# The last group of each block of an input projection: value columns in place of query columns

## The chip, the cores and the metric

The kernel runs on one core of a Trainium2 chip. The metric is the time of one execution in microseconds (us), measured on the device. A difference is called one if it is more than half a per cent, which is about what a measurement of this kernel can tell from no change.

## What is computed

One layer of a decoder, for 256 tokens of width 4096. The part that matters here is the first large product, the input projection: the modulated tokens `u` times a weight matrix of 4096 rows and 11824 columns.

```
mod = c @ w_ada[l] + b_ada[l]
shift, scale, gate = jnp.split(mod, 3, axis=-1)
u = x * (1.0 + scale[:, None]) + shift[:, None]
proj = u @ w_in[l]
(rg_x, rg_g, nsa_q, kv_c, kv_s, kv_w, nsa_gl, nsa_g,
 hg_q, hg_f, hg_i, hg_g) = jnp.split(proj, splits, axis=-1)
...
y = jnp.concatenate([y_rg, y_nsa, y_hg], axis=-1) @ w_out[l]
x = _layer_norm(ALPHA * x + (1.0 + gate[:, None]) * y, ln_g[l], ln_b[l])
```

The columns of `proj` feed three mixers: a gated recurrence (rg), a sparse attention (nsa; `ks` and `vs`, the halves of `kv_s`, are the keys and values of its selected branch, `nsa_q` its queries) and a linear recurrence (hg). A second product, the output projection, follows, and a layer norm ends the layer.

## The kernel before

**Groups and blocks.** The 4096 rows of the input weights are cut into 32 tiles of 128, and these into ten blocks of 2, 2, 2, 3, 3, 4, 4, 4, 4, 4 tiles (the list `KB`; the text counts blocks 0 to 9). The columns are cut into 46 groups of 256 (one of 304), and the list `GROUPS` sets the order in which every block goes through them: kc, vc, four rg_g, four rg_x, four hg_q, four hg_g, then hg_f and hg_i in turn four times, ks, vs, kw, vw, eight nsa_g, eight nsa_q. A group in a block of n tiles is 6n matmuls on TensorE: two halves, n tiles, and three products, because every fp32 operand is split into a rounded part (`hi`, `uh`) and a rest (`lo`, `ul`). At the end of a group in a block the sum leaves PSUM and is added to the group's sum `acc` in SBUF, by VectorE, or by ScalarE (`ev`) and GpSimd.

**Two layouts.** The last field of a group says how its matmuls are made, in `mm` (line 456). Where it is `"nt"`, the weights are the stationary operand and the tokens move through: `seq = ((wh, uh), (wh, ul), (wl, uh))`. Where it is `"tn"`, the tokens are stationary and the weights move: `seq = ((uh, wh), (uh, wl), (ul, wh))`. Both move 256 columns a matmul. `"tn"` are the four hg_i, vs and vw (304 columns); all other groups are `"nt"`. A row of the profile names the moving operand first: `mm<-uh,hi` is an `"nt"` matmul, `mm<-hi,uh` a `"tn"` one.

**Steps.** `chunks` packs the groups of a block into steps of at most 1024 columns times tiles: four tiles make one group a step, two tiles two groups. A step is one DMA of weights (`raw`), a split into `hi` (ScalarE) and `lo` (GpSimd and VectorE, line 118 for all), and its matmuls. Four buffers each hold raw, `hi` and `lo`, and loads and splits are issued some steps ahead.

**What is woven in.** The modulation vector is computed beside this on VectorE (`ps<-ra,pk,ps`, chunks of `w_ada` by DMA into `ra`), one block ahead, and near the end of each block some 8 to 16 small matmuls (line 394) and a few VectorE operations make the next block's `uh` and `ul`; the block after a change of n needs more of this than its own tiles give time for. In block 9 the work of the mixers (fibers, started by a list of conditions in `run_bg`) is woven in between the matmuls. An attention fiber starts when, among other things, its queries and ks, kw, vs, vw are done. The output projection (line 968) comes after block 9.

Of the kernel before, what the change touches and what calls it, by code (L numbers as in the profile page):

```python
# [45 lines left out]
    + [g for i in range(4) for g in (("hg_f", i, 8752 + 256 * i, 256, "nt"),  # L46
                                     ("hg_i", i, 9776 + 256 * i, 256, "tn"))]
    + [("ks", 0, 4608, 256, "nt"),
       ("vs", 0, 4864, 256, "tn"), ("kw", 0, 5120, 256, "nt"), ("vw", 0, 5376, 304, "tn")]
    + [("nsa_g", i, 5680 + 256 * i, 256, "nt") for i in range(8)]  # L50
    + [("nsa_q", i, 2048 + 256 * i, 256, "nt") for i in range(8)]
)
SILU = ("rg_g", "hg_q", "hg_g", "nsa_g")

# [1347 lines left out]
```

## Time and profile before

| | us |
|---|---|
| median of 3 runs | 1672.43 |
| lowest, highest | 1669.08, 1676.03 |
| profiled execution | 1667.61 |
| its span | 1665.9 |
| TensorE busy in the span | 1605.8 (96%) |
| VectorE, ScalarE, GpSimd busy | 1331.2, 972.0, 954.4 |

The profiled execution is one run that the hardware profiler took; its span, from the first instruction to the last, is 1.7 us shorter than its time, and the time is 4.82 us below the median of the runs. Durations are read from it. Matmuls overlap, so that one shown as 281 ns starts some 118 ns after the one before it; what a matmul costs is the distance from start to start.

### The profile page before, as it was taken

To read this page: it belongs to the slowest core of one execution; us is meant where nothing else is said; L and a number is where in the kernel's file an instruction comes from. 1 tells how busy PE (TensorE), PEld (TensorE's weight loads), DVE (VectorE), ACT (ScalarE), POOL (GpSimd) and SP (SyncE) were. 2 spreads that over 40 slices of the span, in tenths; PEclk is the share of its full clock that TensorE was granted. 3 is DMA by queue.
4 is the path that set the end of the run, shared out by engine and by line. 5 is a ranking of instruction groups with operands and counts; after the bars stand their busy time and mean duration, and the time that the engine had idled before them with its cause. 6 is when DMAs were issued, how large, how long until landed. Compare 5 with 4: busy or idle time off the path is not lost.

```text
span 1665.9 us, 33159 instructions
## 1 busy us (share of the span) xinstructions
PE 1605.8 (96%) x11752; PEld 1506.7 (90%) x11752; DVE 1331.2 (80%) x2301; ACT 972.0 (58%) x1557; POOL 954.4 (57%) x765
## 2 busy tenths in 40 slices
PE   4999999999999999999999999889999999999997
PEld 4999999999999999999999999889988888878884
DVE  5668988789888778787777787899679688968875
ACT  2887666665655555555555566664566565655562
POOL 1478987876655555554554555567543444555555
PEclk9999999999999999999999998999999999999999
DMA  8998989999999898898889886767666666689983
GB/s 283 368 334 315 359 302 333 308 349 352 320 348 333 292 343 311 310 330 318 314 323 320 321 310 210 248 237 258 249 216 244 236 215 210 212 292 366 343 332 137
DMA packets 146486, 491.49 MB, mean 295 GB/s; under 512 B 16264, under 2 KB 17288, under 8 KB 146320
## 3 DMA queue, kind: packets, MB, share of 16 engines
q1 hardware_dynamic: 146320, 489.38, 82.5%
q8 instruction: 92, 1.51, 0.4%
q14 instruction: 74, 0.61, 0.1%
HBM read 485.12 MB, written 4.19 MB: 294 GB/s over the span
## 4 chain that ended last, share of the span: by engine, by line
PE 81%; DVE 10%; DMA 3%; ACT 3%; issue 3%; POOL 0%; SPq 0%; DVEq 0%; ACTq 0%; POOLq 0%
PE mm L456 51%; PE mm L968 21%; DVE ps L118 3%; DVE acc L118 2%; DVE lo L118 2%; DMA ra<-in_w_ada_dram 1%; ACT hi L118 1%; PE ps L707 1%; DVE rgt L118 1%; PE ps L900 1%; PE ps L394 1%; PE ps L791 1%; PE ps L1286 1%; DVE hgA L118 1%; DMA raw<-in_w_in_dram 1%
## 5 line engine op out<-in xcount | busy, mean ns | idle before, releaser
L118 POOL TENSOR_TENSOR lo<-raw,hi 128x576 fp32r<-128x576 f32 (+4 forms) x527 | 707.4, 1344 | 620.3 <-ACT hi L118 594.2
L118 ACT CAST hi<-raw 128x1024 fp32r<-128x1024 f32 (+3 forms) x527 | 528.0, 1002 | 495.1 <-POOL lo L118 232.4
L456 PE MATMUL mm<-uh,hi 128*128 128x256 f32 x2560 | 723.5, 283 | 15.0 <-DVE lo L118 8.9
L456 PE MATMUL mm<-uh,lo 128*128 128x256 f32 x2560 | 717.7, 280 | 1.9 <-DVE lo L118 1.4
L456 PE MATMUL mm<-ul,hi 128*128 128x256 f32 x2560 | 717.4, 280 | 0.0
L118 DVE SCALAR_TENSOR_TENSOR ps<-ra,pk,ps 128x512 f32<-128x512 f32 x744 | 520.4, 727 | 8.3 <-DMA ra<-in_w_ada_dram 2.4
L456 PEld LDWEIGHTS mm<-uh,hi 128*128 128x128 f32 x2560 | 485.0, 189 | 19.2 <-DVE lo L118 11.9
L118 DVE TENSOR_TENSOR lo<-raw,ps 128x448 fp32r<-128x448 f32 (+4 forms) x500 | 303.0, 606 | 233.8 <-ACT ps L118 183.0
L456 PEld LDWEIGHTS mm<-ul,hi 128*128 128x128 f32 x2560 | 488.5, 191 | 0.3 <-issue 0.2
L456 PEld LDWEIGHTS mm<-uh,lo 128*128 128x128 f32 x2560 | 484.6, 189 | 2.6 <-DVE lo L118 1.9
L118 ACT CAST ps<-raw 128x448 fp32r<-128x448 f32 (+4 forms) x500 | 260.1, 520 | 6.8 <-DVE acc L118 6.0
L118 DVE TENSOR_TENSOR acc<-mm,acc 128x512 f32<-128x512 f32 (+1 forms) x346 | 231.1, 668 | 0.0
L968 PE MATMUL mm<-hi,yh 128*128 128x512 f32 x512 | 210.8, 412 | 0.3 <-ACT ev L118 0.3
L968 PE MATMUL mm<-hi,yl 128*128 128x512 f32 x512 | 201.3, 393 | 0.0
L968 PE MATMUL mm<-lo,yh 128*128 128x512 f32 x512 | 200.1, 391 | 0.0
L968 PEld LDWEIGHTS mm<-hi,yh 128*128 128x128 f32 x512 | 96.4, 188 | 23.3 <-issue 5.7
L968 PEld LDWEIGHTS mm<-hi,yl 128*128 128x128 f32 x512 | 96.1, 188 | 21.5
L456 PE MATMUL mm<-hi,uh 128*128 128x256 f32 (+1 forms) x384 | 110.4, 288 | 4.3 <-ACT hi L118 3.0
L968 PEld LDWEIGHTS mm<-lo,yh 128*128 128x128 f32 x512 | 96.5, 188 | 19.2 <-issue 1.2
L456 PE MATMUL mm<-hi,ul 128*128 128x256 f32 (+1 forms) x384 | 108.9, 284 | 0.0
L456 PE MATMUL mm<-lo,uh 128*128 128x256 f32 (+1 forms) x384 | 108.8, 283 | 0.0
L118 POOL TENSOR_TENSOR acc<-ev,acc 128x512 f32<-128x512 f32 x77 | 101.4, 1317 | 2.7 <-ACT ev L118 2.3
(193 smaller groups left out, 1474.6 us busy)
## 6 DMA issues: line engine op xcount, KB each, us to landing
ra<-in_w_ada_dram SPq DMA_DIRECT2D x323, 512.0 KB, 5.5
raw<-in_w_in_dram SPq DMA_DIRECT2D x291, 512.0 KB, 4.8
raw<-in_w_out_dram SPq DMA_DIRECT2D x128, 512.0 KB, 4.7
raw<-in_w_in_dram SPq DMA_DIRECT2D x90, 384.0 KB, 5.0
ra<-in_w_ada_dram SPq DMA_DIRECT2D x64, 384.0 KB, 5.4
ra<-in_w_dram SPq DMA_DIRECT2D x16, 512.0 KB, 3.8
raw<-in_w_ada_dram SPq DMA_DIRECT2D x13, 512.0 KB, 6.1
xz<-in_xz_dram SPq DMA_DIRECT2D x16, 256.0 KB, 5.8
```

What stands on the lines that cost most here:

```text
L118: return f(*a, **k)
L394: nc.tensor.matmul(pp[:, q:q + 1], lhsT=acc[q], rhs=ones[:, 0:1], start=kb > 0, stop=True, skip_group_check=kb == 0)
L456: nc.tensor.matmul(dst, lhsT=l_, rhs=r_, start=s and n_ == 0, stop=e and n_ == 2)
L707: nc.tensor.matmul(pl[:, (2 * x + j) * 64:(2 * x + j + 1) * 64], lhsT=k[:, j, x * P:(x + 1) * P], rhs=qp[:, j, x * P:(x + 1) * P].rearrang ...
L791: nc.tensor.matmul(s1[:, b * T:(b + 1) * T], lhsT=q[:, j, P:], rhs=kk[b][:, g], start=True, stop=True)
L900: nc.tensor.matmul(o, lhsT=v0, rhs=eT[:, 0:2], start=b == 0, stop=False)
L968: nc.tensor.matmul(state[x], lhsT=a_, rhs=b_, start=ci == 0 and j == 0 and n_ == 0, stop=ci == len(part) - 1 and j == 1 and n_ == 2)
L1286: nc.tensor.matmul(pb, lhsT=rows[-1 - x], rhs=rows[i // 2][:, i % 2 * 512:i % 2 * 512 + 512], start=True, stop=True)
```

## The change

In `GROUPS`, vs moves from place 28 of each block to place 46, the last, and the eighth group of queries, nsa_q 7, takes place 28. The rows of all other groups, and all code, stay. The host lays the weights out in the new order, so that the loads stay in line.

```diff
     + [("ks", 0, 4608, 256, "nt"),
-       ("vs", 0, 4864, 256, "tn"), ("kw", 0, 5120, 256, "nt"), ("vw", 0, 5376, 304, "tn")]
+       ("nsa_q", 7, 2048 + 256 * 7, 256, "nt"), ("kw", 0, 5120, 256, "nt"), ("vw", 0, 5376, 304, "tn")]
     + [("nsa_g", i, 5680 + 256 * i, 256, "nt") for i in range(8)]
-    + [("nsa_q", i, 2048 + 256 * i, 256, "nt") for i in range(8)]
+    + [("nsa_q", i, 2048 + 256 * i, 256, "nt") for i in range(7)]
+    + [("vs", 0, 4864, 256, "tn")]
```

Lines behind it are numbered one higher in the changed kernel. On TensorE the two places read as follows; the numbers behind the names are buffers. First the end of the 28th group of block 6 and the start of the 29th, kw, before:

```order
L456 MATMUL mm_9275<-hi_9153,uh_8157 128x256
L456 MATMUL mm_9275<-lo_9154,uh_8157 128x256
L456 MATMUL mm_9275<-hi_9153,ul_8158 128x256
L456 MATMUL mm_9314<-uh_8114,hi_9188 128x256
L456 MATMUL mm_9314<-ul_8115,hi_9188 128x256
L456 MATMUL mm_9314<-uh_8114,lo_9189 128x256
```

The same place in the changed kernel:

```order
L457 MATMUL mm_9275<-uh_8157,hi_9153 128x256
L457 MATMUL mm_9275<-ul_8158,hi_9153 128x256
L457 MATMUL mm_9275<-uh_8157,lo_9154 128x256
L457 MATMUL mm_9314<-uh_8114,hi_9188 128x256
L457 MATMUL mm_9314<-ul_8115,hi_9188 128x256
L457 MATMUL mm_9314<-uh_8114,lo_9189 128x256
```

Before, the layout turned from `"tn"` back to `"nt"` here; now it is `"nt"` on both sides. Second, the end of the last group of block 6 and the start of kc in block 7, before:

```order
L456 MATMUL mm_9996<-uh_8157,hi_9859 128x256
L456 MATMUL mm_9996<-ul_8158,hi_9859 128x256
L456 MATMUL mm_9996<-uh_8157,lo_9860 128x256
L456 MATMUL mm_10031<-uh_9899,hi_9905 128x256
L456 MATMUL mm_10031<-ul_9900,hi_9905 128x256
L456 MATMUL mm_10031<-uh_9899,lo_9906 128x256
```

And in the changed kernel:

```order
L457 MATMUL mm_9996<-hi_9859,uh_8157 128x256
L457 MATMUL mm_9996<-lo_9860,uh_8157 128x256
L457 MATMUL mm_9996<-hi_9859,ul_8158 128x256
L457 MATMUL mm_10031<-uh_9899,hi_9905 128x256
L457 MATMUL mm_10031<-ul_9900,hi_9905 128x256
L457 MATMUL mm_10031<-uh_9899,lo_9906 128x256
```

The turn from `"tn"` to `"nt"` now stands at the border of two blocks. These are the only places that differ, two in each of the ten blocks (the last one leads into the output projection): the rows of VectorE, ScalarE, GpSimd and of the DMA queue are the same, in the same order and of the same shapes, and so are all other rows of TensorE.

## Rows read from the trace of the kernel before

**Rows 1.** The page: busy time by engine, and the chain's shares by engine and line

```profile
PE 1605.8 (96%) x11752; PEld 1506.7 (90%) x11752; DVE 1331.2 (80%) x2301; ACT 972.0 (58%) x1557; POOL 954.4 (57%) x765
...
PE 81%; DVE 10%; DMA 3%; ACT 3%; issue 3%; POOL 0%; SPq 0%; DVEq 0%; ACTq 0%; POOLq 0%
```

**Rows 2.** Windows, blocks 1 to 6, 8 and 9: length, busy us (instructions) by engine, clock, DMA

```profile
core 0: us, PE busy (x) PEld busy (x) DVE busy (x) ACT busy (x) POOL busy (x), PEclk, DMA share, GB/s
103.97:169.49 65.52, 65.52 (x563) 65.52 (x561) 52.77 (x86) 49.25 (x76) 59.82 (x46) 1.00 0.88 320
169.49:240.82 71.33, 68.01 (x566) 66.18 (x565) 65.03 (x123) 48.25 (x75) 63.17 (x49) 1.00 0.93 342
240.82:340.19 99.37, 98.32 (x842) 97.92 (x840) 78.52 (x165) 61.95 (x110) 75.13 (x79) 1.00 0.91 312
340.19:445.81 105.62, 101.30 (x844) 99.53 (x844) 96.06 (x188) 64.60 (x114) 75.06 (x72) 1.00 0.96 347
445.81:574.46 128.65, 128.65 (x1120) 128.65 (x1121) 102.89 (x171) 71.94 (x101) 69.37 (x50) 1.00 0.90 326
574.46:705.02 130.56, 130.56 (x1122) 130.56 (x1121) 101.56 (x169) 70.82 (x98) 66.36 (x47) 1.00 0.90 319
835.57:966.12 130.55, 130.55 (x1122) 130.55 (x1121) 101.45 (x168) 70.99 (x98) 65.95 (x47) 1.00 0.89 319
966.12:1179.90 213.78, 198.06 (x1571) 192.96 (x1570) 192.24 (x300) 126.39 (x194) 126.96 (x103) 0.96 0.74 259
```

**Rows 3.** Windows of TensorE in block 6: groups 1-20, 21-22, 23-24, 25-26, 27-28, 29, 30, 31-41, 43-46

```profile
574.47:631.00 56.53, 56.53 (x482) 1.00 0.92 331
631.00:636.46 5.46, 5.46 (x51) 1.00 1.01 371
636.46:642.12 5.66, 5.66 (x51) 1.00 0.86 293
642.12:647.57 5.45, 5.45 (x50) 1.00 0.87 306
647.57:653.23 5.66, 5.66 (x50) 1.00 0.83 290
653.23:655.96 2.73, 2.73 (x26) 1.00 0.92 338
655.96:659.29 3.33, 3.33 (x27) 1.00 0.91 341
659.29:689.21 29.92, 29.92 (x267) 1.00 0.89 317
...
693.63:705.02 11.39, 11.39 (x98) 1.00 0.86 291
```

**Rows 4.** The same in block 5: groups 2-20, 21-22, 27-28, 29, 30, 31-41

```profile
448.67:500.35 51.68, 51.68 (x459) 1.00 0.96 354
500.35:506.00 5.65, 5.65 (x50) 1.00 1.01 378
...
517.12:522.57 5.45, 5.45 (x50) 1.00 0.85 284
522.57:525.40 2.83, 2.83 (x26) 1.00 0.91 336
525.40:528.73 3.33, 3.33 (x26) 1.00 0.91 362
528.73:558.66 29.93, 29.93 (x267) 1.00 0.87 316
```

**Rows 5.** The same in block 4, its groups 34 to 37 (nsa_g 3 to 6)

```profile
414.40:422.88 8.48, 8.48 (x74) 1.00 0.97 365
```

**Rows 6.** Who waited for whom on TensorE, block 4 to the start of block 5: total, times, longest

```profile
PE mm L456 <- DVE lo L118: 4.2, 6, 2.2
```

**Rows 7.** Windows, parts of blocks 2 and 4, columns as in rows 2

```profile
169.49:205.00 35.51, 34.82 (x291) 33.78 (x290) 34.66 (x65) 24.26 (x36) 34.20 (x27) 1.00 1.00 378
...
380.00:410.00 30.00, 27.86 (x224) 26.49 (x223) 29.79 (x62) 16.27 (x29) 19.73 (x17) 1.00 0.95 337
```

**Rows 8.** Timeline of TensorE: the first matmuls of an attention fiber (start, length)

```profile
1220.24 0.96 PE L841 MATMUL ps<-kcT,acc 128*128 128x15 f32 x8
```

## The prediction

> **What bounds the kernel now.** I read the page first, then windows cut at the blocks, then windows cut at the groups. The page says that TensorE is busy for 96% of the span and carries 81% of the chain that ended last [rows 1]. The windows say where that is strict: in blocks 1, 5, 6 and 8 (block 7 repeats 6) TensorE is busy for the whole window, 130.56 of 130.56 us in block 6, while VectorE has 101.56 and the DMA engines are busy nine tenths [rows 2]. There, time is the number of matmuls times their pace, and nothing else. In blocks 2, 4 and 9 TensorE has holes (71.33 against 68.01, 105.62 against 101.30, 213.78 against 198.06).
>
> Now the pace. Blocks 5 and 6 do the same work, and one takes 128.65 us, the other 130.56 [rows 2], both without a hole and at a granted clock of 1.00, which is the level of 2.4 GHz. The windows by groups show why. A window also counts matmuls that reach into it, so I divide by what the groups hold, 24 matmuls each at four tiles. In block 6 groups 1 to 20 take 56.53 us, which is 56.53/480 = 117.8 ns a matmul; groups 31 to 41 take 29.92 us, which is 29.92/264 = 113.3 ns [rows 3]. So the same instruction has two paces, 4.44 ns apart; I call them slow and fast. The rows also say when it changes. In block 6 the groups go: 1-20 slow, hg_f 1 and hg_i 1 (21-22) fast (5.46 us for 48), 23-24 slow (5.66), 25-26 fast (5.45), ks and vs slow (5.66), kw fast (2.73 for 24). Each change falls right behind a `"tn"` group of 256 columns: behind hg_i 0, hg_i 1, hg_i 2, hg_i 3, vs. Block 5 shows that it is a turn and not a property of the groups: it starts fast (groups 2-20 at 51.68/456 = 113.3 ns), and then every one of these is the other way round, 21-22 slow (5.65), ks and vs fast (5.45), kw slow (2.83) [rows 4]. Two more things set the pace. Behind vw, the group of 304 columns, it is fast in either block, though kw before it was fast in block 6 and slow in block 5 [rows 3, 4]. And behind the small matmuls that end the modulation, inside group 42, it is slow: groups 43-46 take 11.39 us, 96 matmuls at 118 ns and one late start [rows 3]. So block 6 hands the slow pace on to block 7, and groups 1 to 20 there crawl again.
>
> **The change part by part.** No instruction is added or removed on any engine, and no DMA; shapes, order and loads stay. What moves is one turn of the layout.
>
> *At place 28.* ks, nsa_q 7 and kw are now `"nt"` throughout, so the turn behind vs is gone. In a block that starts slow, kw stays slow: 24 × 4.44 ns = 0.11 us lost at four tiles, 0.05 at two. vw behind it takes 3.33 us in both cases [rows 3, 4], and nsa_g starts fast in both.
>
> *At place 46.* Behind the modulation matmuls nsa_q 3 (its rest) to nsa_q 6 and vs are slow as the four groups there were. Then vs is followed by kc of the next block: `"tn"` to `"nt"`, a turn, from slow to fast. The next block starts fast. Then, by the pattern, only hg_f 1, hg_i 1, hg_f 3 and hg_i 3 are slow before the modulation, against 24 slow groups before (1-20, 23, 24, 27, 28). That makes 20 groups of 6n matmuls at 4.44 ns: 2.13 us a block at four tiles, 1.60 at three, 1.07 at two.
>
> *Sum, by blocks.* Block 0 has no block before it: +0.05 (kw). Block 1: -1.07. Block 2 has VectorE busy 34.66 of its first 35.51 us with the DMA engines full [rows 7], so I take 0 for its own groups. Block 3: -1.60. Block 4, VectorE 29.79 of 30 in its middle [rows 7]: 0. Block 5 is fast from its second group already, by a stall: TensorE waited 2.2 us, the longest of six waits for `lo` [rows 6], and came out fast. I take 0, and bounds below. Blocks 6, 7 and 8: -6.39. Block 9: the first five groups, before the mixers' matmuls come between, 120 × 4.44 ns = -0.53; behind them I take nothing, and all 1104 matmuls of it are worth at most 4.9 us either way. In all 0.05 - 1.07 - 1.60 - 6.39 - 0.53 = -9.54 us. The profiled execution has 1667.61, which becomes 1658.07; the median of the runs stands 4.82 higher, so 1662.9, and I say 1663, 0.57% less.
>
> *What costs nothing, and by what cover.* A `"tn"` group wants `lo` at its second matmul instead of its third, one matmul earlier, 0.12 us; it frees `lo` one matmul earlier and `hi` one later. In blocks 1, 5 to 8 TensorE never waits [rows 2], so `lo` is there; uncovered, ten blocks would pay 1.2 us. vs is complete 18 groups later than before. The attention needs it, but its first matmul comes at 1220.24 [rows 8], 40 us behind the end of block 9 at 1179.90 [rows 2], and the order of all rows around it is unchanged: nothing. Faster blocks ask for weights faster: block 5, at 326 GB/s against 319, ran without a hole [rows 2], and its groups 2-20 drew 354 [rows 4]. So the loads keep up with a block that starts fast.
>
> *The rule beside the row.* The rows have two paces for one shape, 113.3 and 117.8 ns, and which one holds depends on what came before [rows 3, 4]. [...]
>
> **The rivals.** *Nothing happens.* The pace depends on columns alone, or the turn at a block's border does not take because the tokens change there too (`uh` is a new buffer). For it: no row shows a `"tn"` group at a border. Against it: the turns within blocks 5 and 6, each in both directions [rows 3, 4]. Then only kw is lost, at most 0.9 us over ten blocks: 1672 to 1673. Chance 0.12.
>
> *The early blocks give it back.* VectorE works through the modulation of blocks 2 and 4 at its own speed [rows 7]; if that work does not begin earlier when block 1 or 3 ends earlier, TensorE meets the same `lo` later and the 2.67 us go into stalls: 1665.6. And a stall leaves the pace open: the one before block 5 ended fast, but now a `"tn"` group stands before it, and if block 5 comes out slow, 19 groups are lost, 2.03 us, and with both it is 1667.6. The same lottery holds for the runs of before, which speaks for a smaller difference on the median. Against it: VectorE has slack in blocks 1 and 3 (52.77 of 65.52, 78.52 of 99.37 [rows 2]), so it follows TensorE there and should begin earlier. Chance 0.27.
>
> *Slower.* vw does not always leave the fast pace: in block 4 nsa_g 3 to 6 took 8.48 us for 72 matmuls, 117.8 ns [rows 5], behind a kw that had waited. If a slow kw leads to slow groups behind vw (now every block that starts slow has one), kw, nsa_g, nsa_q 0 to 2 and most of 3 are slow, 12.9 groups; if the modulation then turns the pace to fast, 4.1 groups gain, vs turns it back to slow, and every block repeats it. That is 8.8 groups net, 0.93 us at four tiles, 0.70 at three, 0.47 at two, 6.5 us over blocks 0 to 8: 1679. It is decided at nsa_g 0 of block 0, the first behind a slow kw. Against it: block 5, slow kw and fast behind [rows 4]. Chance 0.05.
>
> **How the numbers follow.** The forecast, turn at the border and gains kept, has 0.56, and a range of its own of 1658 to 1667: the runs lie from 1.5 to 8.4 us above the profiled execution. Half a per cent is 8.4 us, 1664.1, near the middle of my cases: I give 0.7 of the forecast and 0.3 of the second rival to the far side of it, and 0.02 to a larger gain in block 9, 0.49 in all. Slower by half a per cent needs the third rival and more: 0.04. The rest, 0.47, is within. The range goes from 1657, the forecast with its early blocks gaining a little, to 1671, which takes in the second rival and stops before the first.
>
> **What would show it.** Right: windows of blocks 6, 7 and 8 of 128.4 us instead of 130.56, their groups 1-20 at 54.4 us, 21-22 at 5.66, kw at 2.72, and nsa_g at 113.3 ns; block 1 near 64.5 and block 3 near 97.8. Wrong: blocks 6 to 8 still at 130.6 (the border does not turn), nsa_g at 117.8 ns (vw does not reset), or blocks 2 and 4 longer by what 1 and 3 won. What would break the sum is a stall at a border that ends in the other pace than I think, above all before block 5.

## The result, and the profile after

The changed kernel takes 1661.35 us, median of 8 runs (1655.64 to 1667.87), against 1670.46 for the kernel before, also 8 runs. The ratio is 0.9944, with a 95% interval from 0.9926 to 0.9961: 0.56% faster. A second set of runs on another occasion gave 0.9953 (0.9932 to 0.9974). The forecast was 0.57% and 1663. The 1663 was counted from the first three runs of the kernel before (median 1672.43); from the 1670.46 of all eight the same sum gives 1660.9.

The windows of the profile after, block by block (blocks 1 to 6, 8 and 9; block 7 repeats 6), with the columns of [rows 2]:

```profile
102.87:167.32 64.45, 64.45 (x562) 64.45 (x561) 52.57 (x87) 49.44 (x77) 59.97 (x46) 1.00 0.90 328
167.32:239.77 72.45, 69.40 (x567) 67.83 (x565) 64.89 (x123) 48.13 (x75) 63.02 (x49) 0.98 0.92 337
239.77:336.49 96.72, 96.51 (x842) 96.31 (x840) 77.68 (x165) 62.00 (x110) 75.30 (x79) 1.00 0.92 320
336.49:442.70 106.21, 100.38 (x844) 99.03 (x844) 96.90 (x188) 64.52 (x114) 74.99 (x72) 1.00 0.95 344
442.70:571.23 128.53, 128.53 (x1120) 128.53 (x1121) 102.95 (x171) 71.94 (x101) 69.37 (x50) 1.00 0.90 327
571.23:699.65 128.42, 128.42 (x1122) 128.42 (x1121) 101.65 (x169) 70.83 (x98) 66.40 (x47) 1.00 0.90 325
828.07:956.49 128.42, 128.42 (x1122) 128.42 (x1121) 101.50 (x168) 71.00 (x98) 66.00 (x47) 1.00 0.90 324
956.49:1170.11 213.62, 197.39 (x1570) 191.82 (x1569) 192.25 (x300) 126.34 (x193) 127.11 (x103) 0.96 0.73 258
```

Set beside [rows 2], blocks 6 to 8 lost 2.13 to 2.14 us each, block 1 1.07, block 3 2.65. Blocks 2 and 4, where VectorE is busy nearly throughout [rows 7], grew by 1.12 and 0.59. The output projection begins at 1170.11 us instead of 1179.74. Block 9 ends there, 213.62 us long in both; [rows 2] let its window run on to 1179.90, 0.16 us too far.

The windows of TensorE in block 6 after: groups 1 to 20, 21 and 22, 27 to 29, 31 to 41, 43 to 46:

```profile
571.23:625.65 54.42, 54.42 (x483) 1.00 0.94 343
625.65:631.31 5.66, 5.66 (x51) 1.00 1.00 373
642.42:650.59 8.17, 8.17 (x74) 1.00 0.87 301
653.91:683.84 29.93, 29.93 (x267) 1.00 0.87 316
688.26:699.65 11.39, 11.39 (x98) 1.00 0.83 286
```

Groups 1 to 20, 56.53 us in [rows 3], now take 54.42: 113.4 ns a matmul. Groups 21 and 22 went the other way, 5.46 to 5.66 us. ks, nsa_q 7 and kw are fast, 8.17/72 = 113.5 ns. But for kw it is the picture of block 5 in [rows 4], now in blocks 5 to 8. The granted clock is 1.00 in all these windows, so none of this is the clock.

### The profile page after: what moved, and what is told of

Read it like the earlier page. It is cut to its first block, busy times and chain, and to the rows that moved or that the text cites. A ratio compares the mean times of both kernels' runs of the same rounds, so it can differ in the third digit from the quotient of the medians.

```text
span 1659.1 us, 33161 instructions
## 1 busy us (share of the span) xinstructions
PE 1597.9 (96%) x11752; PEld 1497.6 (90%) x11752; DVE 1331.8 (80%) x2301; ACT 971.6 (59%) x1557; POOL 954.5 (58%) x765
## 4 chain that ended last, share of the span: by engine, by line
PE 79%; DVE 11%; DMA 3%; issue 3%; ACT 3%; POOL 0%; SPq 0%; DVEq 0%; ACTq 0%
PE mm L457 50%; PE mm L969 21%; DVE ps L119 3%; DVE acc L119 2%; DVE lo L119 2%; DMA ra<-in_w_ada_dram 1%; ACT hi L119 1%; DMA raw<-in_w_in_dram 1%; PE ps L708 1%; DVE rgt L119 1%; PE ps L901 1%; PE ps L1287 1%; DVE rgy L119 1%; PE ps L792 1%; PE ps L395 1%
```

## Experiments

In the variants of the kernel, blocks 0 to 8 have an order of their own (a list `BLOCKS08` used in `chunks`), and block 9 keeps the order of before, so that nothing woven into it moves. The diffs show parts of that list. The cause is read from windows of single blocks, in one profiled execution of each variant. Four variants were timed once: 1661.13 us (the change in blocks 0 to 8 alone), 1667.50 (vs first) and 1662.53 (two turns), against 1670.27 for the kernel before, and 1696.21 (without the offset), against 1670.61.

**The change in blocks 0 to 8 alone.**

```diff
-    for g in GROUPS:
+    for g in GROUPS if kb == NKB - 1 else BLOCKS08:
```

> The change in blocks 0 to 8 alone; block 9, with all that is woven into it, has the order of before. My theory (the gain is made at the borders, and block 9's order is worth nothing): blocks 6 to 8 at 128.42 us, block 1 near 64.5, block 9 about 213.6 from a fast start, start of the output projection within 2 us of the changed kernel's 1170.1 us. Rival (part of the gain is from vs and nsa_q 7 having changed places in block 9): the output projection starts later by more than 2 us than in the changed kernel.

Windows of blocks 7 and 9:

```profile
702.78:831.20 128.42, 128.42 (x1122) 1.00 0.92 325
959.62:1173.24 213.62, 201.34 (x1571) 0.93 0.74 259
```

Blocks 6 to 8 and block 9 are as in the changed kernel, to 0.01 us. The output projection began at 1173.24 us, 3.1 us later than in the changed kernel, which by the number is the rival's side. But block 9 is not where the 3.1 us are: block 9 began 3.1 us later already, and blocks 0 to 8 have the changed kernel's order. In this execution the input projection began 1.6 us later (36.62 against 35.01), blocks 3 and 5 were longer (98.96 against 96.72, 130.17 against 128.53) and block 4 shorter (104.53 against 106.21). Blocks 3 and 4 differ by the pace and the stalls, block 5 by the clock behind its stall (see the second profile of the changed kernel, below). Block 9's order is worth nothing here; the bound of 2 us that I had set was narrower than one execution's luck.

**vs first instead of last.**

```diff
+BLOCKS08 = (
+    [("vs", 0, 4864, 256, "tn")]
+    + [("kc", 0, 4096, 256, "nt"), ("vc", 0, 4352, 256, "nt")]
...
+    + [("nsa_q", i, 2048 + 256 * i, 256, "nt") for i in range(0, 8)]
```

> In blocks 0 to 8 vs stands first, ahead of kc, and nsa_q 7 last; block 9 keeps the order of before. The border between blocks is then from "nt" to "tn", and the turn to "nt" comes one group later. My theory (a turn anywhere between the modulation's matmuls and kc makes kc and the 19 groups behind it fast): blocks 6 to 8 take 128.5 us, with vs slow and kc to hg_i 0 at 113.3 ns; block 0 depends on how it starts. Rival (it is the last place, or vs being off the border's new tokens, that counts): 130.4 us or more, kc to hg_i 0 at 117.8 ns.

Windows of block 7, then of its groups 2 to 21:

```profile
704.08:832.61 128.53, 128.53 (x1123) 1.00 0.89 325
...
706.91:761.30 54.39, 54.39 (x482) 1.00 0.94 345
```

128.53, where 128.5 was expected, with vs slow (704.08 to 706.91, 2.83 us) and kc to hg_i 0 at 54.39/480 = 113.3 ns. The last place and the border are not what counts; a turn ahead of kc is. The whole time, 1667.50 us, shows little of it: in this execution block 4 took 108.65 us and block 9, in the order of before, 216.89 instead of 213.62. Why block 9 was longer was not tried.

**Two turns.**

```diff
+                                     ("hg_i", i, 9776 + 256 * i, 256, "tn"))][:7]
...
+    + [("nsa_q", i, 2048 + 256 * i, 256, "nt") for i in range(0, 5)]
+    + [("vs", 0, 4864, 256, "tn")]
+    + [("nsa_q", i, 2048 + 256 * i, 256, "nt") for i in range(5, 7)]
+    + [("hg_i", 3, 9776 + 256 * 3, 256, "tn")]
```

> In blocks 0 to 8 vs stands third but last, behind nsa_q 4, and hg_i 3, the fourth "tn" group of the linear recurrence, is the last group; nsa_q 7 stays where the change put it, and block 9 keeps the order of before. There are then two turns between the modulation and kc. My theory: vs slow, nsa_q 5, nsa_q 6 and hg_i 3 fast, kc to hg_i 0 slow again; blocks 6 to 8 take 130.0 us (23 slow groups and the rest of one, where before had 28 and the rest). Rival (a "tn" group in the last place, or taking vs away from place 28, gives the gain): 128.4 us or less.

Windows of block 7, of its groups 1 to 20, and of its last three:

```profile
701.21:831.23 130.02, 130.02 (x1122) 1.00 0.90 321
...
701.21:757.75 56.54, 56.54 (x482) 1.00 0.94 335
823.06:831.23 8.17, 8.17 (x74) 1.00 0.77 278
```

130.02, where 130.0 was expected; groups 1 to 20 are slow again, and the last three (nsa_q 5, nsa_q 6, hg_i 3) are fast, 8.17/72 = 113.5 ns. A `"tn"` group in the last place, even behind vs moved away from place 28, gives a slow next block if another turn stands before it. So the turns are counted, not the places.

**A bare stream.** The first try at the cause: matmuls alone, with nothing of the layer around them.

```diff
+    nt(40)
+    for _ in range(4):
+        tn()
+        nt(4)
```

> This kernel computes nothing of the layer: it loads one block of tokens and two blocks of weights, splits them, and runs some 3600 matmuls in one stream without a wait behind the first 25, in stretches of "nt" groups (24 matmuls of 256 columns) with one thing put between two stretches: one "tn" group four times, then "tn" groups of 12, 6, 3 and 1 matmuls, two and three "tn" groups in a row, "tn" groups of 304 columns and of 256 in turn, 16 small matmuls of one column three times, and groups whose two operands both come from the weights or both from the tokens. My theory, that a turn from "tn" to "nt" changes the pace by itself: stretches alternate between 113.3 and 117.8 ns a matmul behind each single "tn" group, are at 113.3 behind 304 columns and at 117.8 behind the small ones. Rival, that the turn needs what stands around it in the kernel (semaphore waits of a new step, DMA traffic, evacuations): one pace throughout, the same in every stretch.

Windows of the stretches of 96 `"nt"` matmuls behind the first two `"tn"` groups:

```profile
130.10:141.46 11.36, 11.36 (x98) 1.00 0.00 0
144.30:155.66 11.36, 11.36 (x98) 1.00 0.00 0
```

One pace, 11.36/96 = 118.3 ns, behind every one. My theory fell here: the turn alone does nothing in this stream. (Around the 16 small matmuls the granted clock was lower, 0.91 between 320 and 400 us, so the stretches behind them say nothing.)

**The same with semaphore waits and fresh weights.**

```diff
+    resident(40)
+    fresh(40, False)
+    resident(20)
+    fresh(40, True)
+    resident(20)
```

> As bare_stream, this computes nothing of the layer: four "nt" groups and one "tn" group in turn, without DMA and modulation. It runs 40 groups on resident weights, then 40 whose hi and lo are written anew for each group by ScalarE and VectorE into four buffers (so that each group's matmuls wait for two semaphores, which are there early), then 20 resident, then 40 fresh ones that also change the PSUM bank with every group and are copied out, then 20 resident. In bare_stream, without waits, the pace stayed at 118.3 ns whatever was turned. Theory A, that a turn acts through the semaphore waits at a group's first matmuls: the 40 fresh groups show 113.3 and 117.8 ns in stretches that change behind "tn" groups, the resident ones one pace. Theory B, that it takes the change of PSUM bank or the evacuation: only the second 40 fresh groups show it. Theory C, that it takes more (DMA traffic, the addresses of the kernel): one pace throughout.

Windows of two stretches of 96 `"nt"` matmuls in the first fresh part, a `"tn"` group between them:

```profile
138.80:150.32 11.52, 11.52 (x99) 1.00 0.01 1
153.20:164.72 11.52, 11.52 (x99) 1.00 0.01 1
```

11.52/96 = 120.0 ns, and so in all five parts. Waits, fresh writes, banks and evacuation do not bring two paces forth here, against theories A and B. That alone does not free them in the kernel, whose operands lie elsewhere; the next run does, which has two paces without any of them. But the pace itself was new, 120.0 instead of 118.3, and the two streams differ in where their tiles lie in SBUF. In the kernel the tokens lie 192 bytes off from the weights, by an unused tile:

```
ring.tile([P, SHIFT_W], FT, name="shift", tag="shift", bufs=1)
```

**Ten offsets.**

```diff
+    for i in range(10):
+        token.append(split(ru, f"u{i}", 1))
+        sb.tile([P, 16], FT, name=f"pad{i}")
...
+    for U in token:
+        resident(U)
```

> As bare_stream_waits, nothing of the layer: "nt" groups with a "tn" group after every third, resident weights, no waits. In the two bare streams so far the pace was one, 118.3 and 120.0 ns, and no turn changed it, so a turn needs something else of the kernel. The kernel places its tokens 192 bytes off from its weights (modulo 1024, by the unused tile that SHIFT_W = 48 words leaves); bare_stream_waits had them at 0. Here the same 20 groups run ten times with the tokens 0, 64, 128, ... 576 bytes off, and once more at 192 with hi and lo written anew for each group. Theory C1, that the two paces belong to the place of the operands in SBUF: 120.0 throughout at 0, and at 192 stretches of 113.3 and 117.8 that change behind each "tn" group. Rival C2 (it takes DMA traffic or what else runs in the kernel): 118 to 120 at every offset, no change at a turn.

Windows of the three `"nt"` groups, 72 matmuls, behind successive `"tn"` groups; first at offset 0 (two rows), then at 64 (three), 128 (two) and 192 bytes (four):

```profile
26.07:34.70 8.63, 8.63 (x74) 1.00 0.00 0
37.59:46.23 8.64, 8.64 (x75) 1.00 0.00 0
...
83.31:91.47 8.16, 8.16 (x75) 1.00 0.00 0
94.30:102.78 8.48, 8.48 (x74) 1.00 0.01 2
105.51:113.67 8.16, 8.16 (x74) 1.00 0.01 2
139.24:147.79 8.55, 8.55 (x75) 1.00 0.01 2
150.63:159.18 8.55, 8.55 (x74) 1.00 0.01 2
...
195.59:204.08 8.49, 8.49 (x75) 1.00 0.01 2
206.91:215.08 8.17, 8.17 (x75) 1.00 0.00 0
217.80:226.28 8.48, 8.48 (x74) 1.00 0.00 0
229.11:237.28 8.17, 8.17 (x74) 1.00 0.01 2
```

At offset 0 all are at 8.64/72 = 120.0 ns. At 128 all are at 8.55/72 = 118.8. At 64 and at 192 they alternate between 8.16 and 8.48 us, 113.3 and 117.8 ns, with one `"tn"` group between: the kernel's two paces, in a stream with almost no DMA (share 0.01), no waits and nothing else. Offsets 256 to 576 repeat 0, 64, 128, 192, 0, 64. At 192 with hi and lo written anew, the first of four turns left the pace as it was, and the other three turned it. Only the tokens were moved in this run: it does not tell the offset between tokens and weights from the place of the tokens alone.

**The changed kernel without the offset.**

```diff
-    ring.tile([P, SHIFT_W], FT, name="shift", tag="shift", bufs=1)
```

> The changed kernel without the unused tile of 192 bytes, so that tokens and weights lie at the same offset. Theory C1: all 256-column groups at one pace, 120.0 ns, no turn seen; blocks 6 to 8 take some 134.8 us (45 groups of 24 matmuls at 120.0, vw 3.4 us, modulation 1.8 us), and the kernel some 35 to 55 us more than the changed one. Rival C2: blocks 6 to 8 at 128.4 us with slow and fast groups as in the changed kernel.

Windows of block 7 and of its groups 1 to 20:

```profile
723.37:858.09 134.72, 134.72 (x1122) 1.00 0.87 310
723.37:780.97 57.60, 57.60 (x483) 1.00 0.92 326
```

134.72 us, where some 134.8 were expected, with 57.60/480 = 120.0 ns a matmul. The whole time is 1696.21 us, 33 more than the changed kernel's median of another set (1663.05), a little under the 35 to 55 expected. The two paces belong to the place of the operands.

**vs right behind the modulation.**

```diff
+    + [("nsa_q", i, 2048 + 256 * i, 256, "nt") for i in range(0, 4)]
+    + [("vs", 0, 4864, 256, "tn")]
+    + [("nsa_q", i, 2048 + 256 * i, 256, "nt") for i in range(4, 7)]
```

> The changed order in blocks 0 to 8, but vs at place 43, right behind the group in which the modulation's matmuls stand; nsa_q 4 to 6 follow it; block 9 keeps the order of before. My theory: the turn comes three groups sooner, nsa_q 4 to 6 are fast too and kc of the next block with them: blocks 6 to 8 take 128.10 us (128.42 less 3 x 0.107), the median 2 us below that of the changed kernel. Rival (the turn works at a border only): blocks 6 to 8 at 130.4 us.

Window of block 7:

```profile
702.20:830.30 128.10, 128.10 (x1122) 1.00 0.91 326
```

The blocks did what was expected, 128.10. The median, expected 2 us below that of the changed kernel, did not show it: 1662.72 us, ratio 0.9949 (0.9925 to 0.9974), no difference from the changed kernel, whose three blocks have 0.96 us more. A microsecond is below what these runs resolve.

**All "tn" groups but vs together.** A version that the experiments pointed to: no turn before the group of 304 columns.

```diff
+    + [("hg_f", i, 8752 + 256 * i, 256, "nt") for i in range(4)]
+    + [("hg_i", i, 9776 + 256 * i, 256, "tn") for i in range(4)]
+    + [("vw", 0, 5376, 304, "tn")]
...
+    + [("nsa_q", i, 2048 + 256 * i, 256, "nt") for i in range(0, 5)]
+    + [("vs", 0, 4864, 256, "tn")]
+    + [("nsa_q", i, 2048 + 256 * i, 256, "nt") for i in range(5, 8)]
```

> In blocks 0 to 8 the four hg_f come first, then the four hg_i in a row and vw (304 columns) behind them, then ks and kw, nsa_g, nsa_q 0 to 4, vs, nsa_q 5 to 7; block 9 keeps the order of before. My theory: with a fast start, no turn comes before vw, and vw goes over to fast at two and four tiles; slow are only the rest of the group with the modulation and vs: blocks 6 to 8 take 127.7 us (128.42 less 7 x 0.107), the median some 3 to 4 us below that of the changed kernel and 0.7 to 0.8% below the kernel before. Rival (a "tn" group behind a "tn" group turns the pace as well, or vw behind a "tn" group does not lead to fast): 127.9 to 129.5 us.

Windows of blocks 7 and 5:

```profile
703.71:831.34 127.63, 127.63 (x1122) 1.00 0.89 327
444.04:576.08 132.04, 132.04 (x1121) 0.99 0.89 317
```

Blocks 6 to 8 take 127.63 us, where 127.7 was expected, every group but vs and the rest of one at the fast pace: `"tn"` behind `"tn"` does not turn it. The median is 1658.27 us, ratio 0.9930 (0.9907 to 0.9954) to the kernel before, the lowest of all. Against the changed kernel's 1663.05 in the same set that is 0.3% less; the two intervals overlap, so that it beats the changed kernel is not shown. In the profiled execution block 5 came out of its stall slow, and for its first group at a lower clock (0.99 over the block), and took 132.04; block 9 took 216.83, as in the run with vs first.

**The changed kernel again.**

> The changed kernel once more beside the two others, for its median on the same chip and a second profile. Blocks 6 to 8 at 128.42 us; blocks 2, 4 and 5 may differ from the first profile, since their stalls leave the pace open. My theory: 0.991 to 0.996 of the kernel before. Rival (the gain is luck of that set of runs): 0.998 or more.

Windows of blocks 4, 5 and 6, and of the first group of block 5:

```profile
337.41:440.74 103.33, 99.39 (x846) 1.00 0.96 351
440.74:570.87 130.13, 130.13 (x1121) 0.99 0.90 323
570.87:699.29 128.42, 128.42 (x1123) 1.00 0.91 325
...
440.74:445.18 4.44, 4.44 (x25) 0.62 0.81 287
```

The ratio is 0.9953, so the gain is not luck. Block 6 repeats to the hundredth; block 4 took 103.33 us here and 106.21 in the first profile, block 5 130.13 and 128.53. Block 5's 1.6 us more are not the slow pace. Behind the wait for `lo` at its border (1.8 us) kc took 4.44 us at a mean granted clock of 0.62, its later matmuls 213 ns apart (the level of 1.2 GHz); from the next group on the block is fast. That is part of the spread of the runs.

## Why the prediction was right, step by step

**Two paces and their turn: right, and shown.** Blocks 6 to 8 were forecast at 128.4 us and measured 128.42; vs_first and two_turns, computed by the same count of turns, came out at 128.53 and 130.02. What the prediction did not have is the condition. It spoke of layouts alone, and the bare streams show that a turn changes nothing unless tokens and weights lie 64 or 192 bytes apart modulo 256. The offset of 192 bytes was there before and after, so that the forecast held without knowing it.

**The sum by blocks: right in the total, partly by terms that cancelled.** Up to the output projection the profiled executions differ by 1179.74 - 1170.11 = 9.63 us; forecast were 9.54. Blocks 1 and 6 to 8 are exact. Block 0 was forecast 0.05 us longer; it was 0.69 shorter, because it came out of its cold start at the fast pace, and 0.41 came before it. Both are luck: in the second profile block 0 was slow again. Block 3 gave 2.65 instead of 1.60, since its stalls before block 4 shrank as well (TensorE's holes there were 99.37 - 98.32 = 1.05 us, now 0.21). Block 9 gave 0.00 instead of 0.53: its first five groups are fast, but what follows waits for VectorE's `lo` as before (6.0 us in all, 5.6 before).

Blocks 2 and 4 took back 1.12 and 0.59, where I had 0. In block 2 that is all that block 1 had won, but not by the stalls of the second rival: TensorE's holes there shrank, from 3.32 us to 3.05, and its busy time grew by 1.39, at a mean granted clock of 0.98 instead of 1.00. Behind a wait of 2.34 us for `acc`, 15 matmuls of nsa_g 0 and nsa_g 1 started 213 ns apart, the level of 1.2 GHz. The windows of these two groups, before and after:

```profile
216.65:219.90 3.25, 3.02 (x25) 1.00 1.02 399
214.54:218.85 4.31, 4.31 (x24) 0.63 1.02 388
```

The prediction has no term for the clock. In block 4 the holes did grow, from 4.32 to 5.83 us, as the second rival has it; in the second profile they were 3.94 and the block took 103.33 us. So this comes and goes, and the total of 9.63 is near the forecast partly by luck: with the same order in blocks 0 to 8, the second profile won 9.99 us up to the output projection and the run with the change in blocks 0 to 8 alone 6.50.

**The tail: not foreseen.** The first profile's span fell by 6.8 us only, because the output projection and the layer norm took 488.94 us instead of 486.16. Up to the last 20 us or so the two executions run in step. Then comes this, in the timeline of TensorE (start, length, the idle time before it), before and after:

```profile
1645.33 0.38 PE L1273 MATMUL ps<-ident,nmean 128*1 128x128 f32 x2 [3.58 <-DVE nmean L118]
1635.72 0.59 PE L1274 MATMUL ps<-ident,nmean 128*1 128x128 f32 x2 [3.58 <-DVE nmean L119]
```

In both, TensorE had waited 3.58 us for `nmean`. The windows from there to the last 20 matmuls, and of these 20, first before, then after:

```profile
1645.33:1651.12 5.79, 4.11 (x8) 0.71 0.12 45
1651.12:1659.97 8.85, 8.85 (x21) 1.00 0.77 291
1635.72:1642.93 7.21, 4.88 (x9) 0.50 0.19 73
1642.93:1653.20 10.27, 10.26 (x21) 0.86 0.61 229
```

The granted clock was low behind the wait in both executions. With the kernel before it was back at 1.00 (2.4 GHz) for the last 20 matmuls; with the changed kernel it stayed at 0.50 (1.2 GHz) until they had begun, and the two windows together are 2.84 us longer. The second profile of the changed kernel spent 486.15 us from the output projection to the end, and its execution took 1657.65 us, against 1658.07 forecast for a profiled execution. So the 2.8 us come and go.

**The rivals.** Nothing happens: it did not come true. At 256 columns and a granted clock of 1.00 the kernels and streams here ran at 113.3, 117.8, 118.3, 118.8 and 120.0 ns, so that the number of columns alone does not set the pace. The Trainium skill, "TensorE: Matmul & The Clock Gate", section "Back-to-back issue gap", gives N/2.4 + 2.5 ns as the warm gap of an isolated matmul of N columns, and says that in a stream of weight loads and matmuls both set the spacing. By the isolated figure 256 columns would take 109.2 ns, an estimate; all the paces of the streams here lie 4 to 11 ns above it.

The early blocks give it back: of its 2.67 us 1.71 came in the first profile, 1.12 of them by the clock and not by stalls.

Slower: half of its mechanism is real. Behind a slow kw, vw led to the fast pace in blocks of two and four tiles (six unstalled cases in these traces; block 5 of [rows 4] is one), and the slow pace stayed in blocks of three tiles, as nsa_g 3 to 6 of block 4 had hinted [rows 5]. The one unstalled case is block 3 of the run with the change in blocks 0 to 8 alone, its kw and its groups 31 to 41, 2.12/18 and 23.32/198 = 117.8 ns:

```profile
299.79:301.91 2.12, 2.12 (x20) 1.00 0.94 338
304.41:327.73 23.32, 23.32 (x201) 1.00 0.87 294
```

It did not decide, since blocks of three tiles mostly start fast now. Why three tiles differ was not tried. What the modulation's matmuls make of a slow pace is open too: two of six cases came out fast.

**The free edits: right.** No wait appeared in blocks 1 and 5 to 8, and the attention began 40 us behind the input projection as before.

**What stays open.** Why the place of the operands makes several paces was not tried. It looks like the reads of the moving and the stationary operand getting in each other's way, and it is only argued that they do. On that the Trainium skill, "TensorE: Matmul & The Clock Gate", section "Step-by-step: what each phase is for", says that two independent read ports feed the two operands and that loading the next weights takes no read bandwidth from the running matmul. No run here shows the ports; what the runs show is that the same stream took 120.0 ns a matmul at offset 0 and 113.3 at 192, so that the place of the operands counts in the time all the same. Nor was it tried whether it is the layout that turns the pace or the offset that comes with it: in a `"tn"` group the operands change parts, so that an offset of 192 becomes 64, and 64 becomes 192, while 0 and 128, where nothing turned, stay what they are.

## What to carry to other kernels

Where TensorE is the bound, divide the time of each stretch by its matmuls before believing in one price for a shape: here 4% lay in a pace that no list of waits shows. Then look for what stands between stretches of different pace, and count it, in both directions. And try the offset between the two operands in SBUF, in steps of 64 bytes; it was worth more here (120.0 against 113.3 to 117.8 ns a matmul; in the changed kernel 1696.21 - 1663.05 = 33 us, from a single run) than the order of the groups. And read the granted clock behind every wait: 15 matmuls at the lower level took back here what a whole block had won.

## What the hardware showed that I had not expected

A matmul of 256 columns, fp32r, at the full granted clock, in tiles of 1024 bytes a row, has a pace that goes with the offset between its operands modulo 256 bytes: 120.0 ns at 0, 118.8 at 128, and at 64 and 192 either 113.3 or 117.8, with a memory of which. That is not the whole rule. Only the tokens were moved to find it, and the first bare stream had an offset of 0 as well (each of its tiles holds 4 rows of 304 words in a partition, 4864 = 19 × 256 bytes, and they lie one behind the other), but ran at 118.3.

A `"tn"` group turns the pace for the group behind at 192; at 64 the `"tn"` group itself already runs at the new pace (2.73 us behind groups of 2.83). A `"tn"` group behind another turned nothing. A stall leaves the pace open: block 5 came out of its stall fast in the first profiled executions before and after, and slow in three of the six other profiles with the offset. It can cost the clock too: in four of these six, and in none of the first two, the first group of block 5 was at the lower level.
